# Feed-forward up by seven products of quarters, hidden rows to down through DRAM, output projection by quarters of the columns

## Chip, cores and metric

One core of a Trainium2 chip runs the whole program. Its engines are TensorE (PE: matmuls; the loading of their weights is shown apart as PEld), VectorE (DVE), ScalarE (ACT), GpSimd (POOL) and SyncE (SP, which here issues the DMAs). The metric is the device time of one execution in microseconds. A profiled execution has a span, from the first instruction to the last, and a time of its own a little longer than that.

## What is computed

One step of a one-layer streaming encoder on 1024 prompt positions and 64 positions of running streams, 1088 columns in all, in float32. The layer is a state-space scan and a differential attention side by side, mixed by gates, and after them a feed-forward with a causal convolution:

```
mix = jax.nn.sigmoid(gate_ssm) * (y_ssm @ p['w_branch_ssm']) + jax.nn.sigmoid(gate_att) * (o @ p['w_branch_attn'])
x = x + mix @ p['w_out']
h = _rmsnorm(x, p['norm_ffn_w']) @ p['w_up']          # (1088, 1024) @ (1024, 5632)
ha, hb = jnp.split(h, 2, axis=-1)                     # 2816 each
hc, ffn_new = _causal_dwconv(ffn_past, ha, p['ffn_conv_w'], p['ffn_conv_b'])   # 3 taps, per channel
x = x + (jax.nn.silu(hc) * hb) @ p['w_down']          # (1088, 2816) @ (2816, 1024)
```

`ffn_new`, the last two rows of `ha`, is an output too. The change concerns these lines only.

## The kernel before

Everything lies transposed: channels on the 128 partitions, the 1088 positions along the free dimension. A model row is KT = 8 blocks of 128 channels; the hidden row is FT = 22 blocks. All big products run in a rounded float32 format (fp32r). To keep the accuracy, each operand is split into a rounded part `hi` and the rest `lo`, and each product is three matmuls: hi x hi, hi x lo and lo x hi (`product`, lines 145 to 150). A split is a copy on ACT (`hi`) and a subtraction on DVE (`lo`). Weights come as blocks of 128 x 1024: `weights` (line 130) loads a block into `w_f` (line 140), and splits it (lines 141 and 142); two buffers of each, and in some stages a third.

The columns are worked in three chunks (`WIDE`): 384, 384 and 320. The results of matmuls gather in PSUM, which has eight banks; `acc` (line 111) hands out banks in turn.

Order on the engines: a planner (the tile framework, with a simulated timeline) puts the instructions of each engine into a fixed order. It goes by the order in which the program names them, and by readiness in its own simulation; `tc.high_priority` moves instructions ahead, among them the loading and splitting of weights. On the chip each engine runs its own list in that order and waits on semaphores. A tile from a pool with `bufs=n` can be written again once the readers of the tile n allocations before have ended.

The stages that matter, after the scan:

- Last branch (line 810). Its products are gated and added on DVE, and split into `mix` (lines 807, 808).
- Output projection and second norm (lines 819 to 847). For each chunk of columns, for each of 8 row blocks m: load x, load and split the block of W_out (so every block is loaded three times), 24 matmuls, add to x (line 831, DVE), store x to DRAM (`x1_sc`), square it (ACT), and add the squares up (line 838, POOL). A matmul with ones (line 840) sums over the partitions, `rstd_of` (line 206) forms the inverse root on ACT and DVE, and lines 845 to 847 scale each block and split it into `x2_hi` and `x2_lo`. Two PSUM banks serve this stage.
- Feed-forward (lines 851 to 914). `hidden(f)` forms hidden block f: block f of W_up (its convolution half) and block FT + f (its gating half), each 3 chunks x 8 k x 3 matmuls, up to five PSUM banks; a copy into a row `pre` that holds the carried columns as well; the convolution (line 882 on ACT, line 884 twice on DVE), SiLU (line 885), the gating and the split into `f_hi`, `f_lo`. After every 4 (at last 3) hidden blocks the down projection takes them up: for each of 8 row blocks and 3 chunks the matmuls over those hidden blocks, and one add into `xa` (line 910), a copy of the stream that stays in SBUF. The last group stores it.

Of the kernel before, what the change touches and what calls it, by code (L numbers as in the profile page):

```python
# [9 lines left out]
F32 = mybir.dt.float32  # L10
# [7 lines left out]
P = 128  # L18
# [9 lines left out]

DFF = 2816
FT = DFF // P  # L30
HALF = T // 2
# [13 lines left out]
QR = 10  # L45
QSQ = 1
BF = 3
UPB = 5
NXR = 4
NSQ = 3  # L50
QUICK = 400
# [24 lines left out]
def hybrid_layer(ctx: ExitStack, tc: tile.TileContext, xT, prm, cst, rope, wvd, win, wbs, wba, wout, wup, wdn,  # L76
# [9 lines left out]
    def scratch(name, shape, dt=F32):  # L86
        return dram.tile(shape, dt, name=name, tag=name)
# [8 lines left out]
    x1_sc = scratch("x1_sc", [D, T])  # L96

    par = cp.tile([P, N_PRM], F32, name="par")
    con = cp.tile([P, 4 * P], F32, name="con")
# [11 lines left out]
    def acc(w):  # L111
        nonlocal at_bank
        pool, n = more
        at_bank = (at_bank + 1) % (n + 2)
        pool, tag = (pool, "mx") if at_bank < n else (pm, "mm")
        t = pool.tile([P, 512], F32, name=tag, tag=tag)
        return t[:, :w]
# [85 lines left out]
        for _ in gen:  # L203
            pass

    def rstd_of(pool, out, mean, w, tag, scale=1.0, top=384):

        t = [pool.tile([P, top], F32, name=f"{tag}{i}", tag=f"{tag}{i}") for i in range(2)]
        u, r = (x[: out.shape[0], :w] for x in t)
        act(u, mean, AF.Ln, bias=eps_t[: out.shape[0]], scale=scale)  # L210
        act(r, u, AF.Exp, scale=-0.5)
# [587 lines left out]
    dq.release()  # L799


    mix_pool = tc.alloc_tile_pool(name="mixp", bufs=1)
    mix = [mix_pool.tile([P, KT, T], R32, name=f"mix{i}") for i in range(2)]

    def mixed(m, c, t):
        q = slice(c, c + t.shape[1])
        S.copy(mix[0][:, m, q], t)
        V.tensor_tensor(out=mix[1][:, m, q], in0=t, in1=mix[0][:, m, q], op=ALU.subtract)
# [6 lines left out]
    x2_pool = tc.alloc_tile_pool(name="x2", bufs=1, side="right")  # L815
    x2_hi = x2_pool.tile([P, KT, T], R32, name="x2_hi")
    x2_lo = x2_pool.tile([P, KT, T], R32, name="x2_lo")
    psf = ctx.enter_context(tc.tile_pool(name="psf", bufs=1, space=PSUM))
    with tc.tile_pool(name="op", bufs=1) as op:
        for c, w in WIDE:  # L820
            cs = slice(c, c + w)
            x1 = []
            s1_t = op.tile([P, 384], F32, name="s1", tag="s1")[:, :w]
            for m in range(KT):
                x = op.tile([P, 384], F32, name="x1", tag="x1", bufs=11)[:, :w]
                x1.append(x)
                load(out=x, in_=xT[:, m, cs])
                w_hi, w_lo = weights(wout[m], KT, P)
                ps = acc(w)
                product(ps, [(w_hi[:, k], w_lo[:, k], mix[0][:, k, cs], mix[1][:, k, cs]) for k in range(KT)])  # L830
                V.scalar_tensor_tensor(x, ps, 0.5, x, ALU.mult, ALU.add)
                load(out=x1_sc[P * m : P * (m + 1), cs], in_=x)
                if m == 0:
                    act(s1_t, x, AF.Square)
                else:
                    sq = op.tile([P, 384], F32, name="sq", tag="sq", bufs=2)[:, :w]
                    act(sq, x, AF.Square)
                    G.tensor_tensor(out=s1_t, in0=s1_t, in1=sq, op=ALU.add)
            ps = psf.tile([P, 512], F32, name="st2", tag="st2")[:, :w]
            PE.matmul(ps, ones, s1_t, start=True, stop=True)  # L840
            rs = op.tile([P, 384], F32, name="rs", tag="rs")[:, :w]
            rstd_of(op, rs, ps, w, "n2", 1.0 / D)
            for k in range(KT):
                xr = op.tile([P, 384], F32, name="xr", tag="xr", bufs=2)[:, :w]
                V.scalar_tensor_tensor(xr, x1[k], col(O_FFN + k), rs, ALU.mult, ALU.mult)
                S.copy(x2_hi[:, k, cs], xr)
                V.tensor_tensor(out=x2_lo[:, k, cs], in0=xr, in1=x2_hi[:, k, cs], op=ALU.subtract)
    mix_pool.release()


    extra = tc.alloc_tile_pool(name="wx2", bufs=1)
    with tc.tile_pool(name="fq", bufs=1) as fq, tc.tile_pool(name="fp", bufs=1) as fp:
        ffn_o = fq.tile([P, FT, 4], F32, name="ffn_o")
        xa = fp.tile([P, KT, T], F32, name="xa")
        for m in range(KT):
            load(out=xa[:, m], in_=x1_sc[P * m : P * (m + 1), :])

        def up(block):
            w_hi, w_lo = weights(block, KT, P)
            for c, w in WIDE:  # L860
                ps = psf.tile([P, 512], F32, name="up", tag="up", bufs=UPB)[:, :w]
                product(ps, [(w_hi[:, k], w_lo[:, k], x2_hi[:, k, c : c + w], x2_lo[:, k, c : c + w]) for k in range(KT)])
                yield ps, c, w

        def hidden(f):
            pre = fq.tile([P, FPADW], F32, name="fpre", tag="fpre")
            G.memset(pre[:, 0:2], 0.0)
            G.tensor_copy(pre[:, TP + 2 : TP + 4], par[:, O_FS + 2 * f : O_FS + 2 * f + 2])
            value = up(wup[FT + f])
            early = []  # L870
            for ps, c, w in up(wup[f]):
                n = min(w, TP - c)
                S.copy(pre[:, 2 + c : 2 + c + n], ps[:, :n])
                if n < w:
                    S.copy(pre[:, TP + 4 :], ps[:, n:])
                if f == 0:
                    early.append(next(value))
            G.tensor_copy(ffn_o[:, f, 0:2], pre[:, TP : TP + 2])
            G.tensor_copy(ffn_o[:, f, 2:4], pre[:, FPADW - 2 :])
            cc = fq.tile([P, FCONVW], F32, name="fcc", tag="fcc", bufs=2)  # L880
            cw = lambda i: col(O_FW + 3 * f + i)
            act(cc, pre[:, :FCONVW], AF.Identity, bias=col(O_FB + f), scale=cw(0))
            for i in range(1, 3):
                V.scalar_tensor_tensor(cc, pre[:, i : i + FCONVW], cw(i), cc, ALU.mult, ALU.add)
            act(cc, cc, AF.Silu)
            hi = fp.tile([P, T], R32, name="f_hi", tag="f_hi", bufs=5)
            lo = fp.tile([P, T], R32, name="f_lo", tag="f_lo", bufs=5)
            for ps, c, w in chain(early, value):
                n = min(w, TP - c)
                for o, d, m in ((0, c, n), (n, TP + 2, w - n)):  # L890
                    if m:
                        t = cc[:, d : d + m]
                        V.tensor_tensor(out=t, in0=t, in1=ps[:, o : o + m], op=ALU.mult)
                        S.copy(hi[:, c + o : c + o + m], t)
                        V.tensor_tensor(out=lo[:, c + o : c + o + m], in0=t, in1=hi[:, c + o : c + o + m], op=ALU.subtract)
            return hi, lo

        k0 = 0
        for n in DOWN:
            hid = [hidden(k0 + i) for i in range(n)]  # L900
            for mp2 in range(4):
                o = 1024 * k0 + 256 * n * mp2
                w_hi, w_lo = weights(wdn[:, o : o + 256 * n], n, 256)
                for u in range(2):
                    m = 2 * mp2 + u
                    for c, w in WIDE:
                        ps = acc(w)
                        product(ps, [(w_hi[:, i, P * u : P * (u + 1)], w_lo[:, i, P * u : P * (u + 1)],
                                      hid[i][0][:, c : c + w], hid[i][1][:, c : c + w]) for i in range(n)])
                        V.tensor_tensor(out=xa[:, m, c : c + w], in0=xa[:, m, c : c + w], in1=ps, op=ALU.add)  # L910
                        if k0 + n == FT and m == KT - 1:
                            load(out=yT[P * m :, c : c + w], in_=xa[:, m, c : c + w])
                    if k0 + n == FT and m < KT - 1:
                        load(out=yT[P * m : P * (m + 1), :], in_=xa[:, m])
            k0 += n
        load(out=ffn, in_=ffn_o)
    extra.release()
    x2_pool.release()
    wp.release()


def pack(inputs):
# [20 lines left out]
    wd = A["w_down"][0]  # L943
    parts, k0 = [], 0
    for n in DOWN:
        s = wd[P * k0 : P * (k0 + n)].reshape(n, P, 4, 256).transpose(1, 2, 0, 3)
        parts.append(s.reshape(P, -1))
        k0 += n
    x = np.concatenate([A["x_prompt"][0], A["x_sample"][0]], 0)
# [72 lines left out]
```

## Time and profile before

| | us |
|---|---|
| median of 3 runs (2556.44 to 2561.44) | 2558.32 |
| the profiled execution | 2556.26 |
| its span | 2554.2 |
| output projection, from the first `mix` product to the first of up | 99.7 |
| feed-forward, from there to the last matmul | 784.5 |

The profile lists busy time per engine, as a share of the span, and in 40 equal slices. TensorE's matmuls overlap one another, so the busy time of one of them is longer than its distance to the next. A group row tells line, engine, operation, tile names with their shapes and the count, then the busy time in us and the mean of one in ns, then the idle time of the engine just before, and what ended it. A timeline row has start, duration, engine, line, operation; xN means N instructions merged.

### The profile page before, as it was taken

The numbers are of one execution on the slowest core, as the hardware profiler recorded it, in microseconds if no ns is written. First come the engines' busy times: TensorE is split into PE (matmuls) and PEld (weight loads), VectorE is DVE, ScalarE is ACT, GpSimd is POOL, SyncE is SP. The second block draws the span as 40 slices with busy tenths as digits, with TensorE's granted clock in tenths as the row PEclk, the third lists the DMA queues.
The fourth block names the chain that finished last, engine by engine and source line by source line (L and its number), as shares of the span: only waits on it lengthen the run. The fifth ranks groups of instructions, "written<-read, shape, count | busy, mean of one in ns | idle before, by whom it ended". The sixth has DMA issues, their size and how long they took to land.

```text
span 2554.2 us, 40801 instructions
## 1 busy us (share of the span) xinstructions
PE 2515.7 (98%) x15924; PEld 2435.1 (95%) x15924; DVE 1370.8 (54%) x2359; ACT 1075.7 (42%) x2283; POOL 288.3 (11%) x393
## 2 busy tenths in 40 slices
PE   8999999999999999999999899999999999999999
PEld 7999999999999999997989789999999999999999
DVE  6326255855877577446666754656433333333333
ACT  6234343654665455357655544145313122221221
POOL 3000000100111010015333220022000000000000
PEclk9999999999999999999999999999999999999999
DMA  5217167545445444266696645665311111111112
GB/s 164 82 55 285 52 241 217 168 137 153 123 129 162 114 130 130 69 210 202 205 352 204 210 135 191 196 200 177 117 42 50 42 50 42 49 43 40 44 44 78
DMA packets 216353, 340.42 MB, mean 133 GB/s; under 512 B 28224, under 2 KB 164672, under 8 KB 216032
## 3 DMA queue, kind: packets, MB, share of 16 engines
q1 hardware_dynamic: 216160, 337.81, 41.7%
q8 instruction: 125, 2.05, 0.3%
q14 instruction: 68, 0.56, 0.1%
HBM read 237.60 MB, written 100.13 MB: 132 GB/s over the span
## 4 chain that ended last, share of the span: by engine, by line
PE 71%; DMA 4%; ACT 3%; DVE 2%; issue 1%; SPq 1%; POOL 0%; ACTq 0%; DVEq 0%; POOLq 0%
PE mm L148 13%; PE mm L150 13%; PE mm L149 13%; PE up L150 7%; PE up L148 7%; PE up L149 7%; PE po L582 3%; PE sc L535 1%; PE sc L534 1%; PE pt L563 1%; DMA b_f<-y_sc 1%; PE mx L148 1%; PE yi L697 1%; PE mx L150 1%; PE mx L149 1%
## 5 line engine op out<-in xcount | busy, mean ns | idle before, releaser
L148 PE MATMUL mm<-xn_hi,w_hi 128*128 128x384 f32 (+1 forms) x1416 | 469.9, 332 | 0.9 <-DVE zr L430 0.9
L150 PE MATMUL mm<-xn_hi,w_lo 128*128 128x384 f32 (+1 forms) x1416 | 467.7, 330 | 0.4 <-DVE w_lo L142 0.4
L149 PE MATMUL mm<-xn_lo,w_hi 128*128 128x384 f32 (+1 forms) x1416 | 466.5, 329 | 0.0
L142 DVE TENSOR_TENSOR w_lo<-w_f,w_hi 128x1024 fp32r<-128x1024 f32 (+2 forms) x196 | 242.2, 1236 | 315.2 <-ACT w_hi L141 314.7
L141 ACT CAST w_hi<-w_f 128x1024 fp32r<-128x1024 f32 (+2 forms) x196 | 203.8, 1041 | 444.6 <-PE mm L149 278.7
L148 PE MATMUL up<-x_hi,w_hi 128*128 128x384 f32 (+1 forms) x1056 | 344.3, 326 | 0.0
L149 PE MATMUL up<-x_lo,w_hi 128*128 128x384 f32 (+1 forms) x1056 | 344.2, 326 | 0.0
L150 PE MATMUL up<-x_hi,w_lo 128*128 128x384 f32 (+1 forms) x1056 | 343.1, 326 | 0.0
L148 PEld LDWEIGHTS mm<-xn_hi,w_hi 128*128 128x128 f32 x1416 | 266.2, 188 | 5.3 <-issue 2.0
L150 PEld LDWEIGHTS mm<-xn_hi,w_lo 128*128 128x128 f32 x1416 | 266.1, 188 | 2.9 <-issue 0.8
L149 PEld LDWEIGHTS mm<-xn_lo,w_hi 128*128 128x128 f32 x1416 | 266.2, 188 | 1.8 <-issue 0.6
L148 PEld LDWEIGHTS up<-x_hi,w_hi 128*128 128x128 f32 x1056 | 198.2, 188 | 0.1
L149 PEld LDWEIGHTS up<-x_lo,w_hi 128*128 128x128 f32 x1056 | 198.2, 188 | 0.0
L150 PEld LDWEIGHTS up<-x_hi,w_lo 128*128 128x128 f32 x1056 | 198.1, 188 | 0.1
L910 DVE TENSOR_TENSOR xa<-xa,mm 128x384 f32<-128x384 f32 x144 | 76.5, 532 | 197.2 <-PE mm L150 197.2
L149 PE MATMUL mm<-f_lo,w_hi 128*128 128x384 f32 (+1 forms) x528 | 173.1, 328 | 0.0
L148 PE MATMUL mm<-f_hi,w_hi 128*128 128x384 f32 (+1 forms) x528 | 173.0, 328 | 0.0
L150 PE MATMUL mm<-f_hi,w_lo 128*128 128x384 f32 (+1 forms) x528 | 173.0, 328 | 0.0
L148 PE MATMUL mm<-b_hi,w_hi 128*128 128x384 f32 (+1 forms) x448 | 148.6, 333 | 5.4 <-ACT b_hi L172 3.0
L149 PE MATMUL mm<-b_lo,w_hi 128*128 128x384 f32 (+1 forms) x448 | 147.2, 329 | 2.8 <-DVE b_lo L173 2.8
L150 PE MATMUL mm<-b_hi,w_lo 128*128 128x384 f32 (+1 forms) x448 | 146.7, 328 | 0.5 <-DVE w_lo L142 0.5
L459 DVE SCALAR_TENSOR_TENSOR cc<-pre,par,cc 128x384 f32<-128x384 f32 (+1 forms) x216 | 126.5, 586 | 24.0 <-ACT cc L457 18.9
(270 smaller groups left out, 5073.0 us busy)
## 6 DMA issues: line engine op xcount, KB each, us to landing
w_f<-in_win_dram SPq DMA_DIRECT2D x76, 512.0 KB, 4.0
w_f<-in_wup_dram SPq DMA_DIRECT2D x44, 512.0 KB, 3.6
bc<-a_sc SPq DMA_DIRECT2D x32, 512.0 KB, 6.3
w_f<-in_wout_dram SPq DMA_DIRECT2D x24, 512.0 KB, 3.7
x_sc<-cc SPq DMA_DIRECT2D x48, 192.0 KB, 2.0
kh_t<-k_st SPq DMA_DIRECT2D x32, 272.0 KB, 8.3
kl_t<-k_st SPq DMA_DIRECT2D x32, 272.0 KB, 7.3
w_f<-in_wbs_dram SPq DMA_DIRECT2D x16, 512.0 KB, 4.2
```

Of the source, the lines that this page charges most:

```text
L141: S.copy(hi, w)
L142: V.tensor_tensor(out=lo, in0=w, in1=hi, op=ALU.subtract)
L148: PE.matmul(ps, a_hi, b_hi, start=i == 0, stop=False)
L149: PE.matmul(ps, a_hi, b_lo, start=False, stop=False)
L150: PE.matmul(ps, a_lo, b_hi, start=False, stop=i == n - 1)
L459: V.scalar_tensor_tensor(cc[:, :m], pre[:, i : i + m], cw(i), cc[:, :m], ALU.mult, ALU.add)
L534: PE.matmul(ps[:n, a : a + b], lhs, r_hi, start=True, stop=False)
L535: PE.matmul(ps[:n, a : a + b], lhs, r_lo, start=False, stop=True)
L563: PE.transpose(pt[:kw, (b - b0) * P : (b - b0) * P + n], pr[1][:n, b * P : b * P + kw], ident[:n, :n])
L582: PE.matmul(po[:n, :P], a_t[b // 4][:kw, b % 4 * P : b % 4 * P + n], rhs, start=b == 0, stop=b == nb - 1)
L697: PE.matmul(yi[u : u + 64, e // 2, :L], xdt[:L, e], bc[:L, e, :L], start=True, stop=True)
L910: V.tensor_tensor(out=xa[:, m, c : c + w], in0=xa[:, m, c : c + w], in1=ps, op=ALU.add)
```

## The change

Up. For each pair of row blocks (f and FT + f) the product is a 2 x 2 block product: the weights have two row blocks and two halves of k (512 each), the operand two halves of k and two halves of the columns (544 each). It is formed with seven products of quarters in place of eight (Winograd's form of Strassen's algorithm). The right-hand operands (the quarters b11, b21, b22 and the differences t1 to t4) are formed and split once, after the norm. The left-hand ones are formed for every pair (`left_parts`): the two weight blocks are loaded, POOL forms four sums and differences of 512 columns, and seven operands are split. A half of the columns is two sides of 272; a pile is 12 matmuls of 272 columns, and a pair has 14 piles. Three of the seven products add to a bank that another one has left its sum in, after that sum has been read.

Rows to down. A finished hidden block is stored to DRAM (`h_sc`) in two halves, unsplit, and loaded again and split (`hidden_row`) into the SBUF units that the right-hand operands leave. Down comes after all of up, in groups of 8, 6 and 8 hidden blocks. The stream isn't kept in SBUF: each group loads a chunk, adds to it and stores it to the next DRAM buffer.

Output projection. The columns are worked in quarters of 272. Blocks of W_out are loaded once for the quarters 0 and 1 together, once for quarter 2 and once for 3. Norms and operand differences follow the quarters they need. Five more PSUM banks serve all of this.

```diff
-DOWN = (4, 4, 4, 4, 3, 3)
+DOWN = (8, 6, 8)
+QW = T // 4
+RW = 2 * QW + 4
+ROWS = dict(fa=8, fb=8, fu=4, fs=2, fp=2, fh=2)
+PARTS = ("b11", "t2", "b21", "t3", "t1", "t4", "b22")
...
     def mixed(m, c, t):
+        w = t.shape[1]
+        for q in range(c // QW, -(-(c + w) // QW)):
+            a, b = max(c, QW * q), min(c + w, QW * (q + 1))
+            hi, lo = (u[:, m % 4, a - QW * q : b - QW * q] for u in mix[q][m // 4])
+            S.copy(hi, t[:, a - c : b - c])
+            V.tensor_tensor(out=lo, in0=t[:, a - c : b - c], in1=hi, op=ALU.subtract)
...
+    more = psf, 5
...
+    def output(m, quarters):
+        w_hi, w_lo = weights(wout[m], KT, P)
+        for q in quarters:
...
+            load(out=x, in_=xT[:, m, cs])
+            ps = acc(QW)
+            product(ps, [(w_hi[:, k], w_lo[:, k], *(u[:, k % 4] for u in mix[q][k // 4])) for k in range(KT)])
+            V.scalar_tensor_tensor(x, ps, 0.5, x, ALU.mult, ALU.add)
+            load(out=x1_sc[P * m : P * (m + 1), cs], in_=x)
...
+                act(sq, x, AF.Square)
+                G.tensor_tensor(out=sums[q], in0=sums[q], in1=sq, op=ALU.add)
+
+    def norm(q):
...
+        for k in range(KT):
+            x = x1[q][k // 2][:, k % 2]
+            V.scalar_tensor_tensor(x, x, col(O_FFN + k), rs, ALU.mult, ALU.mult)
+
+    def differences(s, eng):
+
+        b11, b21, b12, b22 = x1[s][:2], x1[s][2:], x1[2 + s][:2], x1[2 + s][2:]
+        t2 = [couple(row("fs", "t2")) for _ in range(2)]
+        for j in range(2):
+            eng.tensor_tensor(out=b11[j], in0=b12[j], in1=b11[j], op=ALU.subtract)
+        for j in range(2):
+            V.tensor_tensor(out=t2[j], in0=b22[j], in1=b11[j], op=ALU.subtract)
+        part("t2", s, t2)
+        for j in range(2):
+            G.tensor_tensor(out=b12[j], in0=b22[j], in1=b12[j], op=ALU.subtract)
+        part("t1", s, b11)
+        part("t3", s, b12)
+        for j in range(2):
+            V.tensor_tensor(out=b21[j], in0=b21[j], in1=t2[j], op=ALU.subtract)
+        part("t4", s, b21)
+        part("b22", s, b22)
+
+    def left_parts(f):
...
+            w = wp.tile([P, WMAX], F32, name="w_f", tag="w_f", bufs=2)
+            load(out=w[:, :1024], in_=wup[f + r * FT])
...
+        G.tensor_tensor(out=s1, in0=q21, in1=q22, op=ALU.add)
+        G.tensor_tensor(out=s2, in0=s1, in1=q11, op=ALU.subtract)
+        def own(src):
+            hi, lo = (row("fa", n, R32)[:, :512] for n in ("wh", "wl"))
+            split(hi, lo, src)
+            return hi, lo
+        yield own(q11)
+        yield own(s2)
+        yield own(q12)
+        G.tensor_tensor(out=q21, in0=q11, in1=q21, op=ALU.subtract)
+        yield own(q21)
...
+        G.tensor_tensor(out=s2, in0=q12, in1=s2, op=ALU.subtract)
...
+    for m in range(KT):
+        output(m, (0, 1))
+    for q in range(2):
+        norm(q)
+        part("b11", q, x1[q][:2])
+        part("b21", q, x1[q][2:])
+    for m in range(KT):
+        output(m, (2,))
+    norm(2)
+    differences(0, G)
+    for m in range(KT):
+        output(m, (3,))
+    ready = list(left_parts(0))
+    norm(3)
+    differences(1, V)
...
+    def hidden_row(r):
...
+            load(out=t, in_=h_sc[P * r : P * (r + 1), 2 * QW * j : 2 * QW * (j + 1)].rearrange("p (a t) -> p a t", a=2))
+            split(hi[:, 2 * j : 2 * j + 2], lo[:, 2 * j : 2 * j + 2], t)
...
+    SIDES = [(p, s) for p in range(7) for s in range(2)]
+    FIRST = [(p, s) for p in (0, 2) for s in range(2)] + [(p, s) for s in range(2) for p in (1, 3, 4, 5, 6)]
+    for f in range(FT):
+        coming, after = left_parts(f + 1) if f + 1 < FT else iter(()), []
...
+        def pile(key, p, s, start):
+            if start:
+                banks[key, s] = acc(QW)
+            ps, w, b = banks[key, s], ready[p], B[PARTS[p], s]
+            for k in range(4):
+                c = slice(P * k, P * (k + 1))
+                for i, (x, y) in enumerate(((0, 0), (0, 1), (1, 0))):
+                    PE.matmul(ps, w[x][:, c], b[y][:, k], start=start and k == i == 0, stop=k == 3 and i == 2,
+                              skip_group_check=not start)
...
+        for p, s in FIRST if f == 0 else SIDES:
...
+            if p == 0:
+                S.copy(u1[:, s], pile("a", p, s, True))
+            elif p == 1:
+                V.tensor_tensor(out=u2[:, s], in0=pile("b", p, s, True), in1=u1[:, s], op=ALU.add)
+            elif p == 2:
+                S.copy(pre[0][:, 2 + QW * s : 2 + QW * (s + 1)], pile("a", p, s, False))
...
+                    cc0 = gate(0)
+            elif p == 3:
+                V.tensor_tensor(out=u1[:, s], in0=pile("b", p, s, False), in1=u1[:, s], op=ALU.add)
+            elif p == 4:
+                V.tensor_tensor(out=hb[1][:, qs], in0=pile("c", p, s, True), in1=u1[:, s], op=ALU.add)
+            elif p == 5:
+                V.tensor_tensor(out=hb[0][:, qs], in0=pile("d", p, s, True), in1=u1[:, s], op=ALU.add)
...
+            else:
+                ps = pile("c", p, s, False)
+                for o, d, n in ((0, 2, QW),) if s == 0 else ((0, 2 + QW, 208), (208, 484, 64)):
+                    V.tensor_tensor(out=pre[1][:, d : d + n], in0=ps[:, o : o + n], in1=u2[:, s, o : o + n], op=ALU.add)
+            if s == 1:
+                x = next(coming, None)
...
+                if f + 1 == FT and p < 4:
+                    hid += [hidden_row(len(hid) + i) for i in range(2)]
...
+        put(1, gate(1))
+        ready = after + list(coming)
...
+    for g, n in enumerate(DOWN):
...
+            for c, w in WIDE:
+                x = row("fa", "xa")[:, :w]
+                load(out=x, in_=path[g][P * m : P * (m + 1), c : c + w])
...
+                V.tensor_tensor(out=x, in0=x, in1=ps, op=ALU.add)
+                load(out=path[g + 1][P * m : P * (m + 1), c : c + w], in_=x)
+            if g < 2 and len(hid) < FT and (g == 0 and len(hid) < 14 or g == 1):
+                hid.append(hidden_row(len(hid)))
```

`gate(h)` is the convolution and SiLU of half h (544 or 546 columns) with the operations of before; `put(h, cc)` multiplies on POOL (544 columns, or 480 and 64) and stores the half to `h_sc`.

More of the change, by code (lines that the diff above doesn't have):

```diff
@@ L204, in run, with rstd_of @@
             pass
-    def rstd_of(pool, out, mean, w, tag, scale=1.0, top=384):
-        t = [pool.tile([P, top], F32, name=f"{tag}{i}", tag=f"{tag}{i}") for i in range(2)]
+    def rstd_of(pool, out, mean, w, tag, scale=1.0, top=384, t=None):
+        t = t or [pool.tile([P, top], F32, name=f"{tag}{i}", tag=f"{tag}{i}") for i in range(2)]
         u, r = (x[: out.shape[0], :w] for x in t)
@@ L812, in hybrid_layer @@
     xn_pool.release()
-    x2_pool = tc.alloc_tile_pool(name="x2", bufs=1, side="right")
-    x2_hi = x2_pool.tile([P, KT, T], R32, name="x2_hi")
-    x2_lo = x2_pool.tile([P, KT, T], R32, name="x2_lo")
+    beyond = tc.alloc_tile_pool(name="un2", bufs=1, side="right")
+    rows = tc.alloc_tile_pool(name="rw", bufs=1)
     psf = ctx.enter_context(tc.tile_pool(name="psf", bufs=1, space=PSUM))
[L819 to L828, printed above, removed]
-                ps = acc(w)
[L830 to L916, printed above, removed]
@@ L917, in hybrid_layer, with row @@
-    extra.release()
-    x2_pool.release()
+    more = psf, 5
+    free = [(beyond, f"n{i}") for i in range(12)] + [(units, f"m{q}{h}{x}") for q in range(4) for h in range(2) for x in range(2)]
+    taken = [(n, s) for s, n in ((0, "b11"), (1, "b11"), (0, "b21"), (1, "b21"), (0, "t2"), (0, "t3"), (0, "t1"), (0, "t4"),
+                                 (0, "b22"), (1, "t2"), (1, "t3"), (1, "t1"), (1, "t4"), (1, "b22"))]
+    home = {at: free[2 * i : 2 * i + 2] for i, at in enumerate(taken)}
+    def row(tag, name, dt=F32):
+        return rows.tile([P, RW], dt, name=name, tag=tag, bufs=ROWS[tag])
@@ new lines, in couple, with split @@
+    def couple(t):
+        return t[:, : 2 * QW].rearrange("p (a t) -> p a t", a=2)
+    def split(hi, lo, src):
+        S.copy(hi, src)
+        V.tensor_tensor(out=lo, in0=src, in1=hi, op=ALU.subtract)
+    x1 = [[] for _ in range(4)]
+    sums = [None] * 4
+    B = {}
+    def output(m, quarters):
+        w_hi, w_lo = weights(wout[m], KT, P)
+        for q in quarters:
+            cs = slice(QW * q, QW * (q + 1))
+            if m == 0:
+                sums[q] = row("fp", "s1")[:, :QW]
+            if m % 2 == 0:
+                x1[q].append(couple(row(("fa", "fb")[q % 2], "x1")))
+            x = x1[q][m // 2][:, m % 2]
+            load(out=x, in_=xT[:, m, cs])
[3 more added lines that the diff above has]
+            load(out=x1_sc[P * m : P * (m + 1), cs], in_=x)
+            if m == 0:
+                act(sums[q], x, AF.Square)
+            else:
+                sq = row("fh", "sq")[:, :QW]
+                act(sq, x, AF.Square)
+                G.tensor_tensor(out=sums[q], in0=sums[q], in1=sq, op=ALU.add)
@@ new lines, in norm, with part @@
+    def norm(q):
+        ps = psf.tile([P, 512], F32, name="st2", tag="st2")[:, :QW]
+        PE.matmul(ps, ones, sums[q], start=True, stop=True)
+        rs = rows.tile([P, QW], F32, name="rs", tag="rs", bufs=1)
+        rstd_of(rows, rs, ps, QW, "n2", 1.0 / D, t=[row("fu", "n2") for _ in range(2)])
+        for k in range(KT):
+            x = x1[q][k // 2][:, k % 2]
+            V.scalar_tensor_tensor(x, x, col(O_FFN + k), rs, ALU.mult, ALU.mult)
+    def part(name, s, src):
+        hi, lo = B[name, s] = [unit(*at) for at in home[name, s]]
+        for j in range(2):
+            js = slice(2 * j, 2 * j + 2)
+            split(hi[:, js], lo[:, js], src[j])
@@ new lines, in differences @@
+    def differences(s, eng):
[10 more added lines that the diff above has]
+        part("t3", s, b12)
+        for j in range(2):
+            V.tensor_tensor(out=b21[j], in0=b21[j], in1=t2[j], op=ALU.subtract)
+        part("t4", s, b21)
+        part("b22", s, b22)
@@ new lines, in hybrid_layer @@
+    for m in range(KT):
[13 more added lines that the diff above has]
+    differences(1, V)
+    ffn_o = rows.tile([P, FT, 4], F32, name="ffn_o")
+    def hidden_row(r):
+        name, s = PARTS[r % 14 // 2], r % 2
+        hi, lo = (unit(*at) for at in home[name, s])
+        for j in range(2):
+            t = couple(row("fb", "hr"))
+            load(out=t, in_=h_sc[P * r : P * (r + 1), 2 * QW * j : 2 * QW * (j + 1)].rearrange("p (a t) -> p a t", a=2))
+            split(hi[:, 2 * j : 2 * j + 2], lo[:, 2 * j : 2 * j + 2], t)
+        return [u.rearrange("p a t -> p (a t)") for u in (hi, lo)]
@@ new lines, in hybrid_layer @@
+    load(out=ffn, in_=ffn_o)
+    k0, path = 0, (x1_sc, x2_sc, x3_sc, yT)
+    for g, n in enumerate(DOWN):
+        while len(hid) < min(FT, k0 + n):
+            hid.append(hidden_row(len(hid)))
+        for m in range(KT):
+            o = 1024 * k0 + P * n * m
+            w_hi, w_lo = weights(wdn[:, o : o + P * n], n, P)
+            for c, w in WIDE:
+                x = row("fa", "xa")[:, :w]
+                load(out=x, in_=path[g][P * m : P * (m + 1), c : c + w])
+                ps = acc(w)
+                product(ps, [(w_hi[:, i], w_lo[:, i], *(u[:, c : c + w] for u in hid[k0 + i])) for i in range(n)])
+                V.tensor_tensor(out=x, in0=x, in1=ps, op=ALU.add)
+                load(out=path[g + 1][P * m : P * (m + 1), c : c + w], in_=x)
+            if g < 2 and len(hid) < FT and (g == 0 and len(hid) < 14 or g == 1):
+                hid.append(hidden_row(len(hid)))
+        k0 += n
@@ L919, in hybrid_layer @@
+    rows.release()
+    beyond.release()
+    units.release()
     wp.release()
@@ L945, in pack @@
     for n in DOWN:
[L946 removed]
+        s = wd[P * k0 : P * (k0 + n)].reshape(n, P, 8, P).transpose(1, 2, 0, 3)
         parts.append(s.reshape(P, -1))
```

58 lines of the change are left out of this document (50 added, 8 removed).

## The prediction

> **What bounds the kernel now.** I read the head of the profile page first, then the busy time of two stretches, then the timelines of TensorE, DVE and POOL inside them. The page:
>
> ```profile
> span 2554.2 us, 40801 instructions
> PE 2515.7 (98%) x15924; PEld 2435.1 (95%) x15924; DVE 1370.8 (54%) x2359; ACT 1075.7 (42%) x2283; POOL 288.3 (11%) x393
> PE   8999999999999999999999899999999999999999
> DVE  6326255855877577446666754656433333333333
> ```
>
> TensorE is busy throughout; DVE has over half its time free in the last third, where the change lies. The windows (length, then busy time and count per engine, granted clock, DMA share, GB/s) are the output projection and then feed-forward up and down:
>
> ```profile
> 1666.40:1766.10 99.70, 97.66 (x582) 95.43 (x581) 66.05 (x88) 50.86 (x74) 30.97 (x20) 1.00 0.67 215
> 1766.10:2550.60 784.50, 784.50 (x4756) 784.19 (x4754) 292.71 (x450) 193.08 (x302) 30.87 (x90) 1.00 0.17 55
> ```
>
> Matmuls overlap, so their price is the distance from start to start. TensorE's timeline (start, duration) gives three widths:
>
> ```profile
> 1849.60 0.34 PE L148 MATMUL up<-x_hi,w_hi 128*128 128x384 f32 x1
> ...
> 1857.95 0.31 PE L148 MATMUL up<-x_hi,w_hi 128*128 128x320 f32 x1
> ...
> 1861.46 0.34 PE L148 MATMUL mm<-f_hi,w_hi 128*128 128x384 f32 x1
> 59.56 0.29 PE L148 MATMUL mx<-w_hi,xn_hi 128*128 128x272 f32 x1
> ...
> 67.89 0.29 PE L148 MATMUL mm<-w_hi,xn_hi 128*128 128x272 f32 x1
> ```
>
> 48 matmuls of 384 columns lie between the first two rows: 8.35/48 = 0.1740 us each. 24 of 320 follow: 3.51/24 = 0.1463 us. The value projection has the new width, 272: 66 steps in 8.33 us, 0.1262 us. With these, up before is 2112 x 0.1740 + 1056 x 0.1463 = 522.0 us and down (1056 and 528) 261.0; together 783.0 of the 784.5 us window. The output projection is 384 x 0.1740 + 192 x 0.1463 = 94.9 of 99.7 us. So the feed-forward runs at TensorE's pace to 1.5 us, and the output stage loses 4.8.
>
> **The change part by part.**
>
> Up. Per row pair 2 blocks x 8 k x 3 terms x 3 chunks = 144 matmuls become 7 products x 2 sides x 4 k x 3 terms = 168 of 272 columns: 168 x 0.1262 = 21.2 us a pair, 22 x 21.2 = 466.4 us. Against 522.0: **-55.6**.
>
> Output projection. 576 matmuls become 768 of 272: 96.9 us, **+2.0**. The 4.8 us that this stage loses now go out of the account and come back in the transition below: **-4.8**.
>
> Down keeps its 1584 matmuls and widths: 0. What it gains in work lies beside a row block's 48 x 0.1740 + 24 x 0.1463 = 11.9 us of TensorE. For prices on the other engines (DVE, then POOL, by timeline):
>
> ```profile
> 1719.84 0.55 DVE L831 SCALAR_TENSOR_TENSOR x<-mm,x 128x384 f32<-128x384 f32 x1
> 1720.31 0.55 DVE L847 TENSOR_TENSOR x_lo<-xr,x_hi 128x384 fp32r<-128x384 f32 x1
> 1720.78 1.22 DVE L142 TENSOR_TENSOR w_lo<-w_f,w_hi 128x1024 fp32r<-128x1024 f32 x1
> 1721.91 1.37 DVE L847 TENSOR_TENSOR x_lo<-xr,x_hi 128x384 fp32r<-128x384 f32 x1
> 1723.20 1.13 DVE L845 SCALAR_TENSOR_TENSOR xr<-x,par,rs 128x384 f32<-128x384 f32 x2
> ...
> 1721.28 1.58 POOL L838 TENSOR_TENSOR s<-s,sq 128x384 f32<-128x384 f32 x1 [2.90 <-ACT sq L837]
> ```
>
> DVE advances 0.47 us per 384 columns and 1.13 per 1024; on that line 272 cost 0.35, 512 0.60, 544 0.64. In the fourth row a POOL add holds DVE up: 1.37 instead of 0.55, 0.82 us for a POOL operation of 384 columns. The L831 row reads PSUM and keeps 0.55. The group rows (busy, mean ns):
>
> ```profile
> L838 POOL TENSOR_TENSOR s<-s,sq 128x384 f32<-128x384 f32 x14 | 22.5, 1607 | 175.8 <-ACT sq L837 175.8
> L838 POOL TENSOR_TENSOR s<-s,sq 128x320 f32<-128x320 f32 x7 | 10.0, 1423 | 20.4 <-ACT sq L837 20.4
> L141 ACT CAST w_hi<-w_f 128x1024 fp32r<-128x1024 f32 x30 | 31.5, 1050 | 40.1 <-PE mm L149 15.2 <-DMA w_f<-in_wout_dram 10.7 <-PE mm L150 5.7
> L846 ACT CAST x_hi<-xr 128x384 fp32r<-128x384 f32 x16 | 8.2, 511 | 9.5 <-DVE xr L845 9.5
> L882 ACT ACTIVATE fcc<-fpre,par 128x1090 f32<-128x1090 f32 x22 | 28.7, 1304 | 2.0
> L878 POOL COPY ffn_o<-fpre 128x2 f32<-128x2 f32 x22 | 20.9, 948 | 636.3 <-ACT fpre L873 636.3
> ```
>
> POOL: 1.98 us for 512, 2.07 for 544, 1.88 for 480, 0.7 for 64 on that line. ACT: 0.62 for 512, some 0.65 for 544, 0.42 for 272.
>
> Down's cover, then: per row block DVE has one split (1.13), three adds (1.3) and a reloaded hidden row (2 x 0.64), 3.7 of 11.9 us; ACT 2.4. The DMAs:
>
> ```profile
> w_f<-in_wup_dram SPq DMA_DIRECT2D x44, 512.0 KB, 3.6
> w_f<-in_wout_dram SPq DMA_DIRECT2D x24, 512.0 KB, 3.7
> xa<-x_sc SPq DMA_DIRECT2D x8, 544.0 KB, 7.7
> GB/s 164 82 55 285 52 241 217 168 137 153 123 129 162 114 130 130 69 210 202 205 352 204 210 135 191 196 200 177 117 42 50 42 50 42 49 43 40 44 44 78
> ```
>
> A block moves weights 0.5, stream 0.54 in and 0.54 out, hidden row 0.54 MB: 2.1 MB in 11.9 us, 180 GB/s, where slices of the page reach 352. On SP a store waits for its add, and the next chunk's load and the next weights queue behind it; eight stream buffers and two weight buffers let them run ahead. I take 0. If the cover is gone, the stream's 72 loads would show part of 7.7 us each; with eight in flight about a microsecond, so up to +6 per group; below nothing is excluded, since the 783.0 are already TensorE's. The eight rows that the first group needs load in the last pair's first four products, from rows stored long before.
>
> Up's other engines, per pair of 21.2 us. DVE: seven weight splits of 512 (4.2), nine reads of 272 and two short ones from PSUM (3.6), four convolution steps (2.6): 10.3 us. POOL: four differences of 512 (7.9), the gating (2.07 + 1.88 + 0.7): 12.6, with the two-column copies (up to 0.95 each) some 14. ACT: 4.3 for splits, 1.7 for copies, some 2.7 for convolution and SiLU: under 9. Stalling DVE 0.82/384 per column, POOL's columns add 6.7 us to DVE: 17.0 of 21.2. So nothing but TensorE binds on average.
>
> New waits: product p2 accumulates in the bank that p0 left, so TensorE waits for ACT's copy out of it; p3 and p6 wait for DVE's adds after p1 and p4. In each case three piles of 12 matmuls, 4.5 us, lie between. Behind a late DVE add stand the next splits, behind a late split the next pair's p0; POOL's tiny copies into the second half's rows wait for the last convolution and hold up the differences behind them. The store of the second half ends some 11 us into the next pair (DVE 0.8, ACT 0.65, DVE 1.3 to 2.3, ACT 0.6, POOL 2.6, then a DMA like the 3.6 us one), and its buffer is needed at 13.6. I take 0.14 us a pair, **+3**, twice what a pair loses now (1.5/22). Bounds -1 and +28, an add late by 1.3 us in every pair; the row of now is nearer, because the slack is 4.5.
>
> **Transition, the largest unknown.** Quarters 2 and 3 of the output projection are 24 matmuls per weight block, 3.03 us, while each block is loaded and split again. The nearest rows are the last chunk of now, 3.51 us of TensorE per block:
>
> ```profile
> 1738.93 0.49 DVE L831 SCALAR_TENSOR_TENSOR x<-mm,x 128x320 f32<-128x320 f32 x1 [1.34 <-PE mm L150]
> ...
> 1766.44 0.48 DVE L831 SCALAR_TENSOR_TENSOR x<-mm,x 128x320 f32<-128x320 f32 x1
> ```
>
> Seven periods in 27.51 us: 3.93 a block, so the supply already falls behind. DVE must now do, from the start of quarter 2 until the second side's first new operand is split: two norms of 10 x 0.35 and four parts (12.1), 8 x (1.13 + 0.35) = 11.8, norm and differences of the first side (3.5 + 14 x 0.64 = 12.5), 11.8 again, the first seven weight splits (4.2), and 3.5 + 6 x 0.64 = 7.3: 59.7 us, with POOL's stalls (14 sums, eight long differences) 76.8. TensorE has 2 x 24.2 and nine piles of 1.51: 62.0. Per block DVE and POOL need about 3.6 us in quarter 2 and 4.2 in quarter 3. I take 4.0 and 4.3: 8 x 0.97 + 8 x 1.27 = 17.9 us lost. After the last output product comes a chain, seen now as
>
> ```profile
> 1765.97 0.31 PE L150 MATMUL mm<-mix,w_lo 128*128 128x320 f32 x1
> 1773.10 1.28 ACT L210 ACT_TABLE_LOAD   x1
> 1774.94 1.28 ACT L211 ACT_TABLE_LOAD   x1
> 1778.29 1.01 DVE L845 SCALAR_TENSOR_TENSOR xr<-x,par,rs 128x320 f32<-128x320 f32 x2
> ```
>
> 12.3 us to the first scaled row; then 8 x 0.35 and 6 x 0.64 until the second side's p1 may start: 18.9 us. The nine piles ahead of it cover 13.6: 5.3 lost, and 2 more while the parts follow at DVE's pace. Together **+25**. Low end +5 (only the chain shows, DVE never behind); high end +40 (4.6 us a block, and the weight differences, 4 x 1.98 on POOL, ahead of the chain). I stay nearer the block rows.
>
> The cut pieces in the last branch double 24 copies and subtractions; now DVE idles there and TensorE covers them: 0, at most +1. The tail (last add, last store) is as before.
>
> Sum: -55.6 + 2.0 - 4.8 + 3 + 25 = **-30.4 us**. The profiled execution took 2556.26 us, 2.06 around its span; so 2525.9, and against the median of the runs, which stands 2.1 higher, **2528 us**.
>
> The row with the POOL add has a rule beside it. The Trainium skill, GPSIMD Engine Reference, section 1, says that GpSimd's SBUF interfaces are shared with VectorE, with contention for DVE instructions with two SBUF inputs; the trace agrees (1.37 for 0.55, and no stretch where one input is PSUM). By it the transition's DVE work is the 76.8; without it 59.7, and the sum would be near its low end, -50.
>
> The matmul distance has another. The Trainium skill, TensorE: Matmul & The Clock Gate, section "Wait — 56ns, not 53.3ns?", gives N / 2.4 GHz + 2.5 ns: an estimate of 115.8 ns at 272 where the trace has 126.2, and 162.5 at 384 where it has 174.0. By the rule up would go from 486.6 to 428.1, -58.5 instead of -55.6; the rows decide.
>
> **Rivals.**
> (A) Slower: POOL holds DVE for its whole duration. Then 12.6 + 10.3 = 22.9 us per pair exceed 21.2, 1.7 x 22 = 37 us in place of 3: 2562. For it: seven long POOL operations in every pair where none stood before, and POOL's 1607 ns mean. Against: the POOL row of 1.58 us stretched DVE by 0.82 only. It turns the sign from (30.4 + 3)/22 = 1.5 us a pair.
> (B) The transition costs only its low end: 2508. For it: DVE was busy only 66 of the output stage's 99.7 us, and its reads of PSUM are not stretched; against: 3.93 us a block today.
> (C) The next pair's weight parts come late, POOL's chain of three differences (6 us) behind the 3.6 us load: some 1 us a pair, 2528 + 19 = 2547. Against: the load may start a whole pair ahead.
>
> **How the numbers follow.** Forecast 0.70, A 0.12, B 0.06, C 0.12. 0.2% is 5.1 us, about what a measurement of this kernel tells from no change. Faster: 0.67 of the forecast, B, and 0.08 of C, 0.81; same: 0.02 of the forecast and 0.03 of C, 0.05; slower: A, and 0.01 each of the forecast and of C, 0.14. The forecast alone, transition from 5 to 40 and pairs up to 12, runs from 2508 to 2552; the range 2506 to 2556 adds B and most of C and leaves out A.
>
> **What would show it.** Right: 272-wide matmuls 0.126 us apart in up, 21 to 22 us a pair; down at 11.9 us a block; TensorE's idle time collected between the start of quarter 2 and the end of the first pair, waiting for the weights' low parts and for operand splits. Wrong: pairs of 22.5 us or more, with TensorE waiting for DVE's adds (A) or for the weight parts (C); or no gap at the transition (B).

## The result

The changed kernel takes 2728.88 us against 2557.38 before: a ratio of 1.0665 (95% interval 1.0644 to 1.0687), 171 us slower where 30 us faster was forecast. Times of whole kernels are medians of their executions. One execution of the kernel with five banks below took 8527.77 us; without it the median given there, 2535.78, is 2535.16. The head of the changed kernel's profile page:

```profile
span 2730.0 us, 43497 instructions
PE 2525.2 (92%) x16646; PEld 2397.3 (88%) x16646; DVE 1502.3 (55%) x2607; ACT 1136.1 (42%) x2434; POOL 492.4 (18%) x582
PE   8999999999999999999998999857887887879998
DVE  6334267747776774567677474584544554562321
```

Up to the end of the last branch little has moved: the first output product starts at 1667.8 us, before at 1666.4. From there on the kernel before had TensorE at 9 in every slice; now it has holes nearly to the end, and no other engine is full in its place. The windows show the output projection, then up, then down of the changed kernel (length, then busy time and count of TensorE, its weight loads, DVE, ACT, POOL; granted clock, DMA share, GB/s):

```profile
1667.80:1809.20 141.40, 108.08 (x751) 103.58 (x751) 75.86 (x112) 57.67 (x89) 39.70 (x31) 0.89 0.46 148
1809.20:2437.00 627.80, 513.50 (x3724) 478.34 (x3723) 327.61 (x526) 205.51 (x363) 222.12 (x264) 0.99 0.20 68
2437.00:2726.50 289.50, 269.27 (x1586) 260.40 (x1584) 84.73 (x126) 39.50 (x52) 4.59 (x3) 1.00 0.47 152
```

The three together take 1058.7 us where before they took 884.2. Down, with the same 1584 matmuls as before, takes 289.5 us for the 261.0 that its matmuls need. So something slows the products themselves. TensorE's and DVE's timelines inside one pair of up (start, duration, in brackets the idle time and what ended it) show it:

```profile
2041.03 0.52 PE L984 MATMUL mx<-m,w_hi 128*128 128x272 f32 x2 [0.53 <-DVE hb L1018]
2043.33 0.52 PE L984 MATMUL mx<-m,w_hi 128*128 128x272 f32 x2 [0.54 <-DVE pre L1026]
2045.63 0.52 PE L984 MATMUL mx<-m,w_hi 128*128 128x272 f32 x2 [0.53 <-DVE hb L1018]
```

```profile
2040.54 0.44 DVE L1018 TENSOR_TENSOR hb<-mx,u 128x272 f32<-128x272 f32 x1 [1.80 <-PE mx L984]
2042.83 0.44 DVE L1026 TENSOR_TENSOR pre<-mx,u 128x272 f32<-128x272 f32 x1 [1.51 <-PE mx L984]
2045.13 0.44 DVE L1018 TENSOR_TENSOR hb<-mx,u 128x272 f32<-128x272 f32 x1 [1.86 <-PE mx L984]
```

A pile of 12 matmuls is 1.50 us, but piles follow each other 2.30 us apart: DVE sits idle until the pile ends, reads the bank in 0.44 us, and only then does TensorE begin the next. The two engines take turns, pile by pile, at 0.80 us a turn, and the tile is `mx` each time. The order isn't that of the program either. Of a pair's seven products, p0 to p6, p4 of a side is followed at once by p6 of the same side (lines 1018, 1026), where the program names the other side's p4 and both p5 between. The list of what TensorE waited for in up names the readers of PSUM one after the other, on ACT as on DVE (total us, times, longest):

```profile
PE mx L984 <- DVE u L1009: 18.5, 22, 2.6
PE mx L984 <- ACT u L1007: 16.1, 24, 0.9
PE mx L984 <- DVE pre L1026: 14.2, 24, 0.7
PE mx L984 <- ACT pre L1011: 13.9, 18, 1.3
```

The reason stands in a line that the change leaves as it was. A pool keeps as many buffers for each tag as its `bufs` says, unless the tile names a number of its own. The pool `psf` is opened with `bufs=1`. Before, up had its own tag there, `up`, with `bufs=UPB`, five. Now the extra banks are `acc`'s: `more = psf, 5` makes five turns in seven go to the tag `mx` of `psf`, but the tag has as many buffers as the pool says, one. So 5 of 7 groups of matmuls share a single bank, and with the two of `mm` the products have three banks, not seven. The text ahead of the prediction ("Five more PSUM banks serve all of this") took the constant for the banks.

### The profile page after: what moved, and what is told of

Same layout as the page of the kernel before. It is cut to its first block, busy times and chain, and to the rows that moved or that the text cites. A ratio compares the mean times of both kernels' runs of the same rounds, so it can differ in the third digit from the quotient of the medians.

```text
span 2730.0 us, 43497 instructions
## 1 busy us (share of the span) xinstructions
PE 2525.2 (92%) x16646; PEld 2397.3 (88%) x16646; DVE 1502.3 (55%) x2607; ACT 1136.1 (42%) x2434; POOL 492.4 (18%) x582
## 4 chain that ended last, share of the span: by engine, by line
PE 64%; DVE 7%; ACT 4%; DMA 4%; issue 2%; POOL 1%; SPq 1%; ACTq 0%; DVEq 0%; POOLq 0%
PE mx L984 11%; PE mm L151 9%; PE mm L153 9%; PE mm L152 9%; PE mx L151 4%; PE mm L984 4%; PE mx L153 4%; PE mx L152 4%; PE po L585 3%; PE sc L538 1%; PE sc L537 1%; PE pt L566 1%; DMA b_f<-y_sc 1%; DMA bc<-a_sc 1%; DVE cc L995 1%
## 5 line engine op out<-in xcount | busy, mean ns | idle before, releaser
L144 ACT CAST w_hi<-w_f 128x1024 fp32r<-128x1024 f32 (+2 forms) x152 | 157.4, 1037 | 377.5 <-PE mx L152 279.7
L145 DVE TENSOR_TENSOR w_lo<-w_f,w_hi 128x1024 fp32r<-128x1024 f32 (+2 forms) x152 | 190.5, 1253 | 133.1 <-ACT w_hi L144 132.3
L984 PE MATMUL mx<-n,wh 128*128 128x272 f32 x736 | 148.8, 297 | 49.3 <-ACT u L1007 16.1
L984 PE MATMUL mx<-m,w_hi 128*128 128x272 f32 x760 | 153.6, 297 | 40.1 <-DVE pre L1026 14.2
L984 PEld LDWEIGHTS mx<-n,wh 128*128 128x128 f32 x736 | 114.5, 188 | 63.4 <-ACT u L1007 21.4
L984 PEld LDWEIGHTS mx<-m,w_hi 128*128 128x128 f32 x760 | 119.1, 190 | 53.7 <-DVE hb L1018 15.7
L151 PE MATMUL mx<-m,w_hi 128*128 128x272 f32 (+2 forms) x366 | 118.1, 323 | 30.3 <-DVE x L862 21.1
L551 ACT ACTIVATE p_t<-sc,mx 128x1024 f32<-128x1024 f32 (+5 forms) x144 | 106.0, 738 | 77.0 <-DVE mx L542 36.9
L153 PE MATMUL mx<-m,w_lo 128*128 128x272 f32 (+2 forms) x366 | 115.5, 316 | 8.0 <-DVE w_lo L145 8.0
L152 PE MATMUL mx<-m,w_hi 128*128 128x272 f32 (+2 forms) x366 | 115.3, 315 | 0.0
L984 PE MATMUL mx<-m,w_lo 128*128 128x272 f32 x380 | 109.7, 289 | 0.0
```

What stands on the lines that cost most here:

```text
L144: S.copy(hi, w)
L145: V.tensor_tensor(out=lo, in0=w, in1=hi, op=ALU.subtract)
L151: PE.matmul(ps, a_hi, b_hi, start=i == 0, stop=False)
L152: PE.matmul(ps, a_hi, b_lo, start=False, stop=False)
L153: PE.matmul(ps, a_lo, b_hi, start=False, stop=i == n - 1)
L551: act(p_t[:n, :nk], sc[c][:n, :nk], AF.Exp, bias=mx[:n, c : c + 1], accum_out=dst)
```

## The experiments

**Five banks.** Theory: the single bank. Rival: DVE and POOL hold one another up, so that PSUM is read late in any bank.

```diff
-    psf = ctx.enter_context(tc.tile_pool(name="psf", bufs=1, space=PSUM))
+    psf = ctx.enter_context(tc.tile_pool(name="psf", bufs=5, space=PSUM))
...
-        ps = psf.tile([P, 512], F32, name="st2", tag="st2")[:, :QW]
+        ps = psf.tile([P, 512], F32, name="st2", tag="st2", bufs=1)[:, :QW]
```

> The changed kernel with the pool of the extra PSUM banks at five buffers per tag instead of one (the tag of the norm's sum keeps one), so that the five turns in seven that go to it get five banks. Theory (one bank): in the changed kernel these five turns share a single bank, and each pile of 1.51 us is followed by some 0.79 us in which TensorE waits for the read of the pile before; with five banks a row pair of up falls from 28 us to 21 to 22 us, a block of down from 14.5 to 12 us, and the whole to 2515 to 2545 us. Rival (DVE and POOL hold one another up, so that the reads are late in any bank): pairs stay above 25 us, the whole above 2650 us.

Measured: 2535.78 us, a ratio of 0.992 to the kernel before (0.9908 to 0.9933). 193 us are gone, and the change is faster after all, by 0.8%. The profile is from the same kernel run again:

> The kernel with five banks once more, for its profile beside the others on one chip: 2532 to 2542 us; in up 800 matmuls of 272 per 100 us and no wait for a PSUM read; the remaining idle time of TensorE between the third quarter of the output projection and the end of the first pair.

It took 2537.96 us in this one execution. Its windows of the three stages:

```profile
1667.30:1784.50 117.20, 101.10 (x753) 98.45 (x751) 74.93 (x111) 56.58 (x88) 38.37 (x30) 0.96 0.56 177
1784.50:2270.50 486.00, 472.69 (x3723) 471.23 (x3723) 341.41 (x522) 205.01 (x363) 253.04 (x264) 0.99 0.26 87
2270.50:2532.20 261.70, 261.39 (x1586) 261.07 (x1585) 86.76 (x131) 41.22 (x54) 3.75 (x5) 1.00 0.54 169
```

Output projection 24.2 us shorter, up 141.8, down 27.8: 193.8 together, with the same work on every engine. Inside up, one window of each kernel, first with one bank and then with five:

```profile
2000.00:2400.00 400.00, 335.28 (x2460) 313.52 (x2460) 197.18 (x318) 122.44 (x222) 144.27 (x174) 1.00 0.18 61
```

```profile
1860.00:2260.00 400.00, 400.00 (x3189) 400.00 (x3188) 273.66 (x424) 162.11 (x291) 213.70 (x229) 1.00 0.25 84
```

400/2460 = 0.163 us a matmul, 27.3 us a pair; 400/3189 = 0.1254 us, 21.1 a pair. TensorE doesn't idle, while DVE is busy for 68% and POOL for 53%, more than with one bank. The rival falls.

**Three buffers**, the same edit with 3 for 5:

> The same with three buffers. Theory (one bank): most of the gap closes already, since a read takes 0.44 us and a pile 1.51 us, but a pair that keeps up to eight sums open has to reorder; 2530 to 2600 us, between the kernel with five and the one with one. Rival (DVE and POOL): as with one bank, above 2650 us.

2537.95 us, a ratio of 0.9924 (0.991 to 0.9939): not told apart from five. With the two of `mm`, five banks in all are enough here.

**One extra bank, in turn with the two others.** The same three banks as in the changed kernel, used evenly:

```diff
-    more = psf, 5
+    more = psf, 1
```

> The changed kernel with its three banks (two and one), but in even turns: the constant that sends five turns in seven to the one extra bank is set to one in three. Theory A (the uneven turns are the fault, three banks would do, since a read of 0.44 us lies within the two piles of 3 us in the other banks): 2540 to 2600 us. Theory B (the number is the fault: a pair keeps up to eight sums open, and with three banks the order must be changed so that sums that follow one another share a bank): above 2640 us.

2546.76 us, 0.995 (0.9934 to 0.9966): theory A holds. The same three banks, used evenly, win back 182 of the 193 us (2728.88 - 2546.76), so the fault is that five turns in seven go to one of them; three in even turn lose only some 9 to 11 us to seven. Its window in up:

```profile
1860.00:2260.00 400.00, 399.16 (x3164) 397.07 (x3163) 267.27 (x417) 157.61 (x282) 197.75 (x225) 1.00 0.24 81
```

**One bank in the kernel before.** No seven products, no POOL work; only up's banks are cut. The early gating products of the first hidden block go, since they hold banks open.

```diff
-UPB = 5
+UPB = 1
...
-                if f == 0:
-                    early.append(next(value))
```

> The kernel before with one PSUM bank for up instead of five, and so without the early gating products of the first hidden block. Theory (one bank): 132 groups of 24 matmuls each wait for the read of the group before, some 0.8 us each, 105 us: about 2660 us, with no POOL work and no seven products in it. Rival (DVE and POOL): the engines' load is unchanged, within 15 us of 2558 us.

2704.75 us, 1.058 (1.0562 to 1.0598). The single bank alone makes the kernel before 147 us slower, 1.1 us for each of 132 groups; the expectation had 0.8, and where the rest comes from wasn't looked into. TensorE waits for the reads of PSUM:

```profile
PE up L148 <- DVE fcc L891: 54.3, 54, 1.5
PE up L148 <- ACT fpre L875: 29.8, 22, 1.4
PE up L148 <- ACT fpre L873: 23.6, 32, 2.7
```

**The transition.** With five banks, output projection and up take 603.2 us where 4464 matmuls at 0.1254 need 559.8: 43 us are lost, nearly all between the third quarter and the end of the first pair. In this window of the kernel with five banks 488 matmuls need 61.2 us of 100:

```profile
1720.00:1820.00 100.00, 72.70 (x488) 69.17 (x487) 81.69 (x116) 55.90 (x89) 37.99 (x28) 0.90 0.34 109
```

The prediction had 25, at most 40, at 0.1262 us a matmul; by that price the loss is 40. Two orders of the quarters were tried on the kernel with five banks, each with 16 loads and splits of W_out's blocks for 24:

```diff
     for m in range(KT):
-        output(m, (0, 1))
+        output(m, (0, 2))
...
-        output(m, (2,))
...
-        output(m, (3,))
+        output(m, (1, 3))
...
-    FIRST = [(p, s) for p in (0, 2) for s in range(2)] + [(p, s) for s in range(2) for p in (1, 3, 4, 5, 6)]
+    FIRST = [(p, s) for s in range(2) for p in (0, 2, 1, 3, 4, 5, 6)]
```

(norm, parts and differences of the first side follow quarters 0 and 2, those of the second 1 and 3; the operands' places are listed in the new order.)

> The kernel with five banks, with the quarters of the output projection taken as 0 and 2 together and then 1 and 3 together: 16 loads and splits of W_out blocks in place of 24, and the first side's seven operands formed while quarters 1 and 3 are multiplied. Theory (the rest of the loss is the transition, where DVE has more to do than TensorE): DVE's work falls under TensorE's 48 us there, what stays is the chain behind the last quarters, 12.3 us and some 10 us of scaling and splitting against 10.6 us of cover; the transition's loss falls from some 43 us to 15 to 20, the whole to 2505 to 2518 us. Rival (the loss is the chain of norm and differences alone, or the first pair's weights): within 8 us of the kernel with five banks, 2528 to 2544 us.

2527.97 us, 0.9881 (0.9865 to 0.9898): faster than with five banks by 8 to 10 us, but 10 above the top of the theory's range, and at the rival's edge, so the time bears out neither. The second order:

```diff
     for m in range(KT):
-        output(m, (2,))
+        output(m, (2, 3))
     norm(2)
     differences(0, G)
-    for m in range(KT):
-        output(m, (3,))
```

> The kernel with five banks, with quarters 2 and 3 taken together and the order otherwise kept: the same 16 loads as with 0, 2 and 1, 3, but both sides' differences behind the last product, with four piles (6 us) of cover. Theory (DVE's volume, mostly the reloaded W_out blocks): saves about 8 x 2 us of DVE and ACT work ahead of the last product and gives part of it back in the chain: 2515 to 2530 us. Rival (the chain decides, the reloads are hidden): 2540 to 2560 us, slower than with five banks.

2527.15 us, 0.9887 (0.9872 to 0.9903): in the theory's range, and level with the order before. But equal times aren't equal waits. What TensorE waits for longest from the output projection on, first with quarters 0, 1 and 2, 3 (in an execution of 2534.9 us, the longest of its four), then with 0, 2 and 1, 3:

```profile
PE mm L982 <- ACT wh L843: 10.1, 1, 10.1
PE mx L982 <- ACT wh L843: 4.9, 1, 4.9
```

```profile
PE mx L153 <- DVE w_lo L145: 6.3, 1, 6.3
```

With 2 and 3 together TensorE stands for the first pair's weight parts, which is what the rival of the run before had named; with 0, 2 and 1, 3 it stands for the split of one block of W_out. So the gain of some 8 us agrees with the reloads saved, but these two runs don't show alone what the reloads cost, nor what the order of the sides is worth. Where the 6.3 us come from shows in the kernel with quarters 0, 2 and 1, 3. DVE's timeline has the scaling of the first and of the next quarter, eight rows each:

```profile
1718.67 3.39 DVE L877 SCALAR_TENSOR_TENSOR x<-x,par,rs 128x272 f32<-128x272 f32 x8
...
1729.57 7.25 DVE L877 SCALAR_TENSOR_TENSOR x<-x,par,rs 128x272 f32<-128x272 f32 x8
```

The second takes twice as long. The kernel with five banks has the same, and a wait of TensorE right behind it:

```profile
1757.60 7.13 DVE L878 SCALAR_TENSOR_TENSOR x<-x,par,rs 128x272 f32<-128x272 f32 x8
1764.65 1.21 DVE L145 TENSOR_TENSOR w_lo<-w_f,w_hi 128x1024 fp32r<-128x1024 f32 x1
```

```profile
1765.91 0.59 PE L153 MATMUL mx<-m,w_lo 128*128 128x272 f32 x1 [6.20 <-DVE w_lo L145]
```

The planner had put eight scaling rows ahead of a weight block's split; TensorE waited 6.20 us for that split. POOL's long differences run at that time. So, in the kernel with quarters 0, 2 and 1, 3, they were moved to DVE:

```diff
-            G.tensor_tensor(out=b12[j], in0=b22[j], in1=b12[j], op=ALU.subtract)
+            V.tensor_tensor(out=b12[j], in0=b22[j], in1=b12[j], op=ALU.subtract)
...
-    differences(0, G)
+    differences(0, V)
```

> The kernel with quarters 0, 2 and 1, 3, with the long differences of the operands that POOL formed (six of 544 columns) moved to DVE. Theory (POOL holds DVE for most of its own time there, so that moving the work costs DVE nothing): DVE takes 0.64 us for each where POOL's 1.5 us held it, 0 to 5 us faster, 2522 to 2528 us. Rival (POOL's work was free): DVE gets 3.8 us more, up to 4 us slower, 2528 to 2532 us. Below 5 us the two can't be told from the time alone; the stretch of the scaling rows (7.25 us for eight where 3.39 is undisturbed) tells.

2521.61 us, 0.986 (0.9843 to 0.9878), the fastest of all. The intervals of this kernel and the one it is an edit of just overlap, so 6 us is not certain from the times. The same eight rows, and the longest wait of TensorE for a split of W_out, are clear:

```profile
1729.10 3.90 DVE L877 SCALAR_TENSOR_TENSOR x<-x,par,rs 128x272 f32<-128x272 f32 x8
```

```profile
PE mm L153 <- DVE w_lo L145: 1.6, 2, 1.0
```

3.90 us in place of 7.25, and a wait of 1.0 us in place of 6.3. Over the whole execution DVE is busy for 1503.7 us against 1505.2, with six operations more: POOL's differences had cost DVE at least as much as they took off it. That agrees with the Trainium skill, GPSIMD Engine Reference, section 1, which says that GpSimd's SBUF interfaces are shared with VectorE, with contention for DVE instructions with two SBUF inputs. The scaling rows have two, `x` and `rs`. What is left of the transition, some 30 us, wasn't taken apart further.

## Why the prediction was wrong

- **The step that failed: "New waits".** It said that between a product and the next one into the same bank "three piles of 12 matmuls, 4.5 us, lie between", and took +3 us, +28 at most. That assumed a bank for each open sum, and it assumed the program's order. With one bank for five turns in seven the three piles don't exist: the planner put the dependent piles one behind the other, and each turn cost 0.80 us. Up lost 627.8 - 486.0 = 142 us by it, and the output projection 24. The prediction never counted the banks, though the listing of the kernel before opens `psf` with one buffer (line 818) and gives `up` its five at the tile (line 861), and the diff touches neither the pool nor `acc`.
- **Down at 0** failed by the same step: +28 us in the changed kernel. With five banks it takes 261.7 us against the 261.0 worked out, so the reloaded rows and the stream through DRAM are hidden, as argued.
- **Up's matmuls** held: 0.1254 us each against 0.1262, 21.1 us a pair against 21.2, once banks are there. By the Trainium skill's N / 2.4 GHz + 2.5 ns (TensorE: Matmul & The Clock Gate, section "Wait — 56ns, not 53.3ns?") the estimate at 272 columns is 115.8 ns. The runs show 125.4.
- **Other engines in up**: DVE 68% and POOL 53% busy with TensorE full, so "nothing but TensorE binds" held, and rival A (POOL holds DVE all the time, 2562 us) is out, though it had the sign. Rival C (weight parts late by 1 us a pair, 2547 us) is out too: with five banks TensorE waits in up, after the first pair, for nothing but one read of 0.7 us. What was to show A, TensorE waiting for DVE's adds, did appear; it proved a bad sign to go by, since any late read of a bank looks like it. ACT's copies in the same list spoke against A.
- **The transition at +25** was mis-sized: by the prediction's own price of a matmul the output projection and up lose 40 us with five banks, where its sum had 25 and 3. POOL's stalls were right in kind and size: eight scaling rows took 3.9 us longer beside the end of one sum and three differences on POOL, and by 0.82 us per 384 columns the three differences alone make 3.5. (The row shown for a read of PSUM, at 1719.84, ran before POOL's add began; in the same trace the one at 1755.60 kept its 0.48 us during an add.) What was missing is that DVE works in a fixed order: a split which TensorE needed next stood behind scaling rows that POOL had doubled, 6.2 us in one piece, so the block rate of 4.0 to 4.3 us was no bound. Rival B (2508 us) is out.
- **The cut pieces of the last branch**, 0 to 1 us: the first output product starts at 1667.8 us and with five banks at 1667.3, before at 1666.4. So little can't be told from the differences between executions.
- **Taken together**: with banks as assumed, the kernel comes to 2535.8 us, 8 above the 2528 forecast and inside its range; most of the excess is the transition's. The arithmetic was of a kernel that had not been written.

## What to carry to other kernels

Count the PSUM buffers that the allocation really gives, tag by tag, before pricing any overlap of matmuls with reads: where a rotation sends consecutive groups to one buffer, every group pays pile, read and turn-around in series (0.8 us per pile of 1.5 here), and a planner rearranges the program around it so that the source's order no longer tells who waits for whom. When the engine that binds gets holes and nobody else is full, look at the tile names in the waits: one name again and again is a buffer short. Elementwise work on POOL isn't free to DVE; next to DVE work with two SBUF inputs it can cost as much as it saves, or more (7.25 us against 3.90 for one stretch here).

## What the runs showed of the hardware

- Three PSUM banks in even turn carry up at TensorE's pace but for 0.8% (3164 against 3189 matmuls in 400 us); five and seven can't be told apart (2537.95 and 2535.78 us).
- Waiting on a single bank costs 1.1 us per group of 24 matmuls in the kernel before, and 0.80 per pile in the changed one, where the read itself takes 0.44.
- Behind the transition's long holes the granted clock falls. In the kernel with five banks, the 4.5 us right behind the wait of 6.20 us show

```profile
1765.90:1770.40 4.50, 4.49 (x20) 4.49 (x21) 4.50 (x5) 2.21 (x5) 2.38 (x2) 0.50 0.49 152
```

  a clock of 0.50 and 20 matmuls, where 36 fit at 0.1254 us. The changed kernel has a stretch of 20 us with TensorE busy for 8.6

```profile
1780.00:1800.00 20.00, 8.60 (x40) 8.41 (x41) 18.11 (x23) 7.86 (x13) 8.75 (x5) 0.62 0.28 93
```

  at a clock of 0.62; in up, where most holes are about half a microsecond, the clock stays at 0.99. So the long holes cost more than their length. A short one in up slows nothing behind it but the pile's first step: from the third matmul on (2041.39 in the pile that begins at 2041.03) they are 0.125 us apart again.
